# S5 recursion over chunks: scans in a rotating frame in place of a stepwise recursion, in a two-layer hybrid encoder

## The chip, the cores and the metric

One core of one Trainium2 chip runs the whole program. The metric is device time in microseconds from launch to the last output, the median of several executions. Engines are TensorE (PE; its weight loads are shown as PEld), VectorE (DVE), ScalarE (ACT), GpSimd (POOL) and SyncE (SP), which issues the DMAs.

## What is computed

Two sequences (a prompt and a sample, 512 tokens of 1024 channels each) pass through the same two layers. Each layer projects to the inputs of four mixers (S5, Hyena, RWKV-7, neighbourhood attention), normalises and projects their outputs, and ends with an MLP.

```python
def encoder_trunk(x, p):
    for l in range(DEPTH):
        h = rms_norm(x, p['ln1_g'][l])
        z = h @ p['w_in'][l]
        z_s5, z_hy, z_rw, z_na = jnp.split(z, IN_SPLITS, axis=-1)
        groups = [rms_norm(y, g) for y, g in (s5_mixer, hyena_mixer, rwkv_mixer, na_mixer)]
        x = x + jnp.concatenate(groups, axis=-1) @ p['w_out'][l]
        h = rms_norm(x, p['ln2_g'][l])
        x = x + jnp.square(jax.nn.relu(h @ p['w_mlp1'][l])) @ p['w_mlp2'][l]
```

(The four calls are shortened.) S5 is a diagonal complex recursion over the tokens, s[t] = a s[t-1] + B u[t], once forwards and once backwards; 16 groups of 16 channels have 64 states each. The pole is a = exp(lambda dt), that is, a magnitude `mag = exp(lam_re dt)` and an angle `lam_im dt`. The output is the real part of C s.

## The kernel before

Tokens lie along the free dimension, channels along the 128 partitions. Dense products (`mm3`, L1385 to L1395) take fp32 operands in two parts and run three matmuls of 128x512 for each pair of tiles: L1392, L1393 and L1394, 9024 in all. Their weights are split by `split` (L297 on ScalarE, L298 on GpSimd or VectorE), and VectorE takes the results from PSUM (L1449, L1518, L1535, L1545).

The program is written as streams of Python generators whose parts are emitted in turn (`together`, `both`). `dense_stream` runs, for layer l and sequence b, the output projection `w_out` of the mixers' outputs, the MLP and `w_in` of the next layer. `rwkv_stream` runs the mixers: for each (l, b) `rwkv` beside `s5`, then `hyena` beside `na`; after (0, 1) come the operators of layer 1 (`prep`: `s5_ops`, `hy_spectra`). The operators of layer 0, and Hyena and attention of (0, 0), are in `first_stream`. `w_out` of (l, b) waits for the mixers of (l, b), and the mixers of (1, b) wait for `w_in` of (1, b). The framework's scheduler sets the order of instructions on each engine at build time, by the priorities of the emission and its own estimate of when operands are ready; on the chip every engine works through its queue in order.

S5 works in chunks of 8 tokens, so a sequence has 64 chunks. `s5_ops` makes the chunk operators of a layer from its weights and keeps them in DRAM (`sB`, `sC`, `GD`), with a^8 in two small tiles (`AR`, `AI`). `s5_front` (L915) loads the inputs `U`, and for each two pairs of groups the operator `Bop` (L926); 32 matmuls (L933) give every chunk's own contribution in PSUM, ScalarE copies it (L935) into `SS` [128, 2 (re, im), 8 pairs, 130], with the forward chunks at places 1 to 64 and the backward ones at 65 to 128. Then 63 steps go over the chunks, all pairs and both directions at once, four VectorE operations on 32 columns each:

```python
        nc.vector.tensor_tensor(out=t2.rearrange("p q (x d) -> p (q x) d", d=2), in0=pv, in1=AIv, op=MUL)
        nc.vector.tensor_tensor(out=t1, in0=pv, in1=ARv, op=MUL)
        t1f = t1.rearrange("p (q x) d -> p q (x d)", q=2)
        nc.vector.tensor_tensor(out=t1f, in0=t1f, in1=t2[:, ::-1], op=ADD)
        nc.vector.tensor_tensor(out=cv, in0=cv, in1=t1, op=ADD)
```

(L946, L947, L949, L950). The halves of `SS` are then exchanged between partitions by two DMAs, and `s5_back` forms the outputs. A front runs four times, once for each (l, b).

## Time and profile before

| | us |
|---|---|
| median of three runs (lowest, highest) | 3235.25 (3233.89, 3237.98) |
| span of the profiled execution, first to last instruction | 3230.3 |
| PE, DVE, ACT, POOL busy in it | 2989.3, 2222.3, 1054.7, 1222.8 |

The profile is of one execution whose own time is not listed apart from the three; its span lies 4.95 us below their median. Busy time of PE counts pipelined matmuls from start to end, so it says less about how far PE is from its best pace than the count of matmuls in a stretch does.

### The profile page before, as it was taken

To read this page: it belongs to the slowest core of one execution; us is meant where nothing else is said; L and a number is where in the kernel's file an instruction comes from. 1 tells how busy PE (TensorE), PEld (TensorE's weight loads), DVE (VectorE), ACT (ScalarE), POOL (GpSimd) and SP (SyncE) were. 2 spreads that over 40 slices of the span, in tenths; PEclk is the share of its full clock that TensorE was granted. 3 is DMA by queue.
4 is the path that set the end of the run, shared out by engine and by line. 5 is a ranking of instruction groups with operands and counts; after the bars stand their busy time and mean duration, and the time that the engine had idled before them with its cause. 6 is when DMAs were issued, how large, how long until landed. Compare 5 with 4: busy or idle time off the path is not lost.

```text
span 3230.3 us, 48385 instructions
## 1 busy us (share of the span) xinstructions
PE 2989.3 (93%) x17328; PEld 2329.1 (72%) x17328; DVE 2222.3 (69%) x4431; ACT 1054.7 (33%) x1934; POOL 1222.8 (38%) x963
## 2 busy tenths in 40 slices
PE   7998898789899998998889999788999999999999
PEld 5676776667677776676667777677777777888887
DVE  8987993774884879648957366868775486544443
ACT  5333233342222334333222233333332233332222
POOL 6644430332323346453333233443333243343333
PEclk9999888799999999998999999899989999999999
DMA  5464253252334334543324333346234333433333
GB/s 162 145 160 151 98 144 93 74 115 77 89 100 143 92 117 140 153 144 93 90 72 106 102 115 108 105 137 167 76 74 117 111 115 101 126 110 98 95 98 108
DMA packets 361397, 365.23 MB, mean 113 GB/s; under 512 B 175014, under 2 KB 215590, under 8 KB 360136
## 3 DMA queue, kind: packets, MB, share of 16 engines
q1 hardware_dynamic: 361160, 362.14, 38.6%
q8 instruction: 140, 2.29, 0.3%
q14 instruction: 97, 0.79, 0.1%
HBM read 305.06 MB, written 54.10 MB: 111 GB/s over the span
## 4 chain that ended last, share of the span: by engine, by line
PE 39%; DVE 14%; DMA 2%; issue 2%; ACT 1%; SPq 1%; POOL 0%; DVEq 0%; ACTq 0%; POOLq 0%
PE pd L1392 10%; PE pd L1394 10%; PE pd L1393 10%; DVE m L1167 1%; DVE m L298 1%; PE ra L675 1%; DVE m L530 1%; PE ra L673 1%; PE ra L467 1%; DVE m L950 1%; DVE m L512 1%; DVE s_t L946 1%; DVE s_t L949 1%; DVE m L1545 1%; DVE do L1535 0%
## 5 line engine op out<-in xcount | busy, mean ns | idle before, releaser
L298 POOL TENSOR_TENSOR m<-m,m 128x512 fp32r<-128x512 f32 x564 | 793.4, 1409 | 1480.2 <-ACT m L297 1432.4
L1392 PE MATMUL pd<-m,m 128*128 128x512 f32 x2984 | 1225.8, 411 | 108.1 <-ACT m L297 36.0
L1394 PE MATMUL pd<-m,m 128*128 128x512 f32 x2984 | 1212.6, 407 | 14.9 <-POOL m L298 9.8
L1393 PE MATMUL pd<-m,m 128*128 128x512 f32 x2984 | 1211.9, 406 | 2.7 <-DVE m L298 2.1
L297 ACT CAST m<-m 128x512 fp32r<-128x512 f32 (+1 forms) x776 | 488.2, 632 | 1112.8 <-PE pd L1393 401.7
L1392 PEld LDWEIGHTS pd<-m,m 128*128 128x128 f32 x2984 | 581.8, 195 | 264.7 <-issue 68.9
L1394 PEld LDWEIGHTS pd<-m,m 128*128 128x128 f32 x2984 | 581.3, 195 | 160.9 <-POOL m L298 16.3
L1393 PEld LDWEIGHTS pd<-m,m 128*128 128x128 f32 x2984 | 581.4, 195 | 132.8 <-issue 9.1
L1545 DVE TENSOR_TENSOR m<-pd,m 128x512 f32<-128x512 f32 x256 | 175.1, 686 | 234.7 <-PE pd L1394 234.1
L298 DVE TENSOR_TENSOR m<-m,m 128x512 fp32r<-128x512 f32 (+1 forms) x212 | 172.6, 814 | 116.6 <-ACT m L297 116.1
L1535 DVE SCALAR_TENSOR_TENSOR do<-pd,R 128x512 f32<-128x512 f32 x128 | 87.7, 687 | 112.5 <-PE pd L1394 104.3
L297 ACT CAST m<-do 128x512 fp32r<-128x512 f32 x128 | 79.4, 620 | 237.2 <-DVE do L1536 237.1
L1167 DVE TENSOR_TENSOR m<-m,m 128x512 f32<-128x512 f32 (+1 forms) x224 | 154.2, 724 | 1.1 <-POOL m L1167 0.8
L298 DVE TENSOR_TENSOR m<-do,m 128x512 fp32r<-128x512 f32 x128 | 101.5, 794 | 45.1 <-ACT m L297 44.5
L1536 DVE TENSOR_TENSOR do<-do 128x512 f32<-128x512 f32 x128 | 129.5, 1013 | 2.6
L467 PE MATMUL ra<-m,m 64*128 64x128 f32 x512 | 73.4, 335 | 22.1 <-DVE m L451 12.4
L467 PEld LDWEIGHTS ra<-m,m 64*128 64x128 f32 x512 | 62.7, 229 | 37.8 <-issue 20.4
L946 DVE TENSOR_TENSOR s_t<-m,s_AI 128x32 f32<-128x32 f32 x252 | 81.6, 324 | 7.3 <-ACT m L935 1.8
L950 DVE TENSOR_TENSOR m<-m,s_t 128x32 f32<-128x32 f32 x252 | 83.1, 330 | 5.0
L675 PE MATMUL ra<-m,m 128*64 128x64 f32 x512 | 79.0, 248 | 0.0
L840 POOL TENSOR_TENSOR m<-m,s5p_i 128x256 f32<-128x256 f32 x64 | 57.8, 903 | 55.0 <-DVE m L842 31.1
L1423 DVE SCALAR_TENSOR_TENSOR m<-m,par,m 128x512 fp32r<-128x512 f32 x64 | 67.4, 1062 | 15.9 <-ACT m L1422 15.8
(351 smaller groups left out, 3609.5 us busy)
## 6 DMA issues: line engine op xcount, KB each, us to landing
m<-in_w_mlp SPq DMA_DIRECT2D x512, 256.0 KB, 2.6
m<-in_w_in SPq DMA_DIRECT2D x176, 256.0 KB, 2.8
m<-zr SPq DMA_DIRECT2D x36, 512.0 KB, 4.0
m<-in_w_out SPq DMA_DIRECT2D x64, 256.0 KB, 2.9
m<-in_xT SPq DMA_DIRECT2D x32, 256.0 KB, 4.3
zr<-do SPq DMA_DIRECT2D x32, 256.0 KB, 2.1
m<-hy_spec SPq DMA_DIRECT2D x8, 1024.0 KB, 5.1
m<-s_sB SPq DMA_DIRECT2D x16, 512.0 KB, 4.2
```

What stands on the lines that cost most here:

```text
L297: self.nc.scalar.copy(out=hi, in_=x)
L298: eng.tensor_tensor(out=lo, in0=x, in1=hi.bitcast(F32), op=SUB)
L467: nc.tensor.matmul(out=pm[q][:, ch - c2, c], lhsT=bk[c][h, ch].rearrange("p a b -> p (a b)"), rhs=ar[c][h, ch].rearrange("p a b -> p (a b) ...
L675: nc.tensor.matmul(out=py[b0:b0 + 64, d, c], lhsT=uv[:, ch, c, q], rhs=sr[:, ch, 2 * c + q], start=st is None, stop=True)
L946: nc.vector.tensor_tensor(out=t2.rearrange("p q (x d) -> p (q x) d", d=2), in0=pv, in1=AIv, op=MUL)
L950: nc.vector.tensor_tensor(out=cv, in0=cv, in1=t1, op=ADD)
L1167: eng.tensor_tensor(out=o, in0=a, in1=b, op=op)
L1392: K.nc.tensor.matmul(out=ps, lhsT=wh, rhs=hh, start=(i == 0), stop=False)
L1393: K.nc.tensor.matmul(out=ps, lhsT=wh, rhs=hl, start=False, stop=False)
L1394: K.nc.tensor.matmul(out=ps, lhsT=wl, rhs=hh, start=False, stop=(i == n - 1))
L1536: nc.vector.tensor_tensor(out=r, in0=r, in1=r, op=MUL)
L1545: nc.vector.tensor_tensor(out=x[m], in0=ps, in1=x[m], op=ADD)
```

## The change

For each layer `s5_ops` now builds two tables. `E` holds the turns exp(i n theta8) for n = 0 to 63, where theta8 is the angle of a^8, built by doubling in six rounds of four products and sums. `rr` holds the magnitude of a^8 at each of 130 places, with zeros where a direction starts. Both go to DRAM as `TD` [128, 8, 386]. `s5_front` works on one pair of groups at a time: it loads `Bop` and the table, runs 16 matmuls (the backward direction with its chunks reversed, so that both directions run upwards), turns the contributions back by their angle straight from PSUM, runs one real scan each for the real and the imaginary part over 130 places, and turns the result forwards again into `SS`. Each pair gives control back to the other streams twice. Comments and docstrings were taken out as well, so lines behind the tables stand 26 lower than before (L1392 is L1418). The core of the diff:

```diff
@@ s5_ops @@
-    x, y = are, aim
-    for _ in range(3):
+    E, rr = M([P, 2, 16, 64]), M([P, 8, 130])
+    x, y = cs, th
+    for i in range(3):
+        last = i == 2
         x2, y2, xy = (K.t([P, 16], "s5p_" + n, 2) for n in ("x2", "y2", "xy"))
         tt(x2, x, x, MUL)
         tt(y2, y, y, MUL)
         tt(xy, x, y, MUL)
-        tt(x2, x2, y2, SUB)
-        V.tensor_scalar(out=xy, in0=xy, scalar1=2.0, scalar2=None, op0=MUL)
+        tt(E[:, 0, :, 1] if last else x2, x2, y2, SUB)
+        V.tensor_scalar(out=E[:, 1, :, 1] if last else xy, in0=xy, scalar1=2.0, scalar2=None, op0=MUL)
+        tt(mag, mag, mag, MUL)
         x, y = x2, xy
-    r8, i8 = pairs(x, y)
...
+    nc.gpsimd.memset(E[:, 0, :, 0:1], 1.0)
+    nc.gpsimd.memset(E[:, 1, :, 0:1], 0.0)
+    for d in range(2):
+        nc.gpsimd.tensor_copy(out=rr[:, :, 1 + 64 * d:65 + 64 * d],
+                              in_=mag.rearrange("p (g d) -> p d g", d=2)[:, d].unsqueeze(2).to_broadcast([P, 8, 64]))
+    nc.gpsimd.memset(rr[:, :, 0:130:129], 0.0)
+    nc.gpsimd.memset(rr[:, :, 1:66:64], 0.0)
+    for k in (1, 2, 4, 8, 16, 32):
+        n = min(k, 63 - k)
+        t1, t2 = M([P, 2, 16, n]), M([P, 2, 16, n])
+        for t, ri in ((t1, 0), (t2, 1)):
+            tt(t, E[:, :, :, 1:1 + n], E[:, ri, :, k:k + 1].unsqueeze(1).to_broadcast([P, 2, 16, n]), MUL)
+        tt(E[:, 0, :, k + 1:k + 1 + n], t1[:, 0], t2[:, 1], SUB)
+        tt(E[:, 1, :, k + 1:k + 1 + n], t1[:, 1], t2[:, 0], ADD)
+        M.free(t1, t2)
+    TD = K.d([P, 8, 386], f"s5_tb{l}")
+    for ri in range(2):
+        nc.sync.dma_start(out=TD[:, :, P * ri:P * ri + P], in_=E[:, ri].rearrange("p (g x) n -> p g (x n)", g=8))
+    nc.sync.dma_start(out=TD[:, :, 256:386], in_=rr)
@@ s5_front @@
-    for gp in range(0, 8, 2):
-        Bop = M([P, 2, 2, 2, P])
...
-        nc.scalar.copy(out=SS[:, :, gp:gp + 2, 1:129], in_=px)
...
+    for g in range(8):
+        Bop = M([P, 2, 2, P])
+        nc.sync.dma_start(out=Bop.rearrange("p r d n -> p (r d n)"), in_=sB[:, g])
+        tb = M([P, 386])
+        nc.sync.dma_start(out=tb, in_=TD[:, g])
+        px = K.p([P, 2, P], "ma")
...
+        E = [tb[:, P * i:P * i + P].unsqueeze(1).to_broadcast([P, 2, P]) for i in range(2)]
+        t = [M([P, 2, P]) for _ in range(2)]
+        W = SS[:, :, g, 1:129]
+        for i in range(2):
+            V.tensor_tensor(out=t[i], in0=px, in1=E[i], op=MUL)
+        V.tensor_tensor(out=W[:, 0], in0=t[0][:, 0], in1=t[1][:, 1], op=ADD)
+        V.tensor_tensor(out=W[:, 1], in0=t[0][:, 1], in1=t[1][:, 0], op=SUB)
+        for ri in range(2):
+            V.tensor_tensor_scan(out=SS[:, ri, g], data0=tb[:, 256:386], data1=SS[:, ri, g], initial=0.0, op0=MUL, op1=ADD)
+        for i in range(2):
+            V.tensor_tensor(out=t[i], in0=W, in1=E[i], op=MUL)
+        for ri, op in ((0, SUB), (1, ADD)):
+            for d, o in ((0, slice(1, 65)), (1, slice(128, 64, -1))):
+                ns = slice(64 * d, 64 * d + 64)
+                V.tensor_tensor(out=SS[:, ri, g, o], in0=t[0][:, ri, ns], in1=t[1][:, 1 - ri, ns], op=op)
+        M.free(tb, *t)
+        for _ in range(2):
+            yield
```

The built program has 3852 VectorE instructions in place of 4434 and the same 13755 on TensorE, but the scheduler gives both, and the DMAs, another order. On VectorE, in the first front, the order before runs steps of the recursion back to back (`m_2613` is `SS`, `s_t` the step's two products, `do` a dense output):

```order
L946 TENSOR_TENSOR s_t_236_2955<-m_2613,s_AI_142_1778 128x32
L947 TENSOR_TENSOR s_t_235_2954<-m_2613,s_AR_141_1777 128x32
L949 TENSOR_TENSOR s_t_235_2954<-s_t_235_2954,s_t_236_2955 128x32
L950 TENSOR_TENSOR m_2613<-m_2613,s_t_235_2954 128x16x2
L946 TENSOR_TENSOR s_t_238_2961<-m_2613,s_AI_142_1778 128x32
L947 TENSOR_TENSOR s_t_237_2960<-m_2613,s_AR_141_1777 128x32
L316 SCALAR_TENSOR_TENSOR do_4413<-dt_4415,par_67,do_4413 128x512
```

In the changed order the first pair of groups stands there (`ma_2682` is the contribution in PSUM, `m_2680` the table, `m_2691` and `m_2692` the products, `m_2653` is `SS`; the order prints a scan as SCALAR_TENSOR_TENSOR):

```order
L965 TENSOR_TENSOR m_2691<-ma_2682,m_2680 128x256
L965 TENSOR_TENSOR m_2692<-ma_2682,m_2680 128x256
L587 COPY m_1903<-ra_1985 32x8x32
L966 TENSOR_TENSOR m_2653<-m_2691,m_2692 128x128
L967 TENSOR_TENSOR m_2653<-m_2691,m_2692 128x128
L969 SCALAR_TENSOR_TENSOR m_2653<-m_2680,m_2653 128x130 x2
L587 COPY m_1903<-ra_1985 32x8x32
L971 TENSOR_TENSOR m_2691<-m_2653,m_2680 128x256
L971 TENSOR_TENSOR m_2692<-m_2653,m_2680 128x256
L298 TENSOR_TENSOR m_4054<-m_4053,m_4052 128x512
L975 TENSOR_TENSOR m_2653<-m_2691,m_2692 128x64 x4
```

Between two pairs of groups the other streams' operations stand, nine rows of them behind this one.

On TensorE, at the end of the mixers of layer 1, sequence 0, the order before has dense products of `w_in` (`pd`) around the sums and broadcasts of the group norms (L271, L293; `ra_16513` and `ra_16532` are those of the mixer that ends last):

```order
L1393 MATMUL pd_18782<-m_18693,m_18776 128x512
L1394 MATMUL pd_18782<-m_18693,m_18778 128x512
L271 MATMUL ra_16513<-c_ones_131,m_16508 128x1 x4
L293 MATMUL nm_18715<-c_eye_129,rsq_ynm_18703 128x128 x4
L1392 MATMUL pd_18826<-m_18511,m_18814 128x512
L1393 MATMUL pd_18826<-m_18511,m_18814 128x512
L1394 MATMUL pd_18826<-m_18511,m_18816 128x512
```

The changed order has, at the same event, the end of attention's values (L1366, L1372), Hyena's last products (L1274), the group norms and the next front's matmuls (L956) with no dense product among them; the last dense product ahead of them is that of `pd_19680`, and the next one, 33 rows further, is the first of `w_out` (`pd_19815`):

```order
L1274 MATMUL ra_15799<-m_15017,m_15673 128x128
L1274 MATMUL ra_15810<-m_15017,m_15673 128x128
L293 MATMUL ma_15666<-c_eye_129,rsq_yma_15654 128x128 x4
L956 MATMUL ma_19891<-m_19864,m_19887 64x64 x8
L956 MATMUL ma_19990<-m_19864,m_19986 64x64 x8
L271 MATMUL ra_15869<-c_ones_131,m_15864 128x1 x4
L956 MATMUL ma_20102<-m_19864,m_20098 64x64 x8
L956 MATMUL ma_20203<-m_19864,m_20199 64x64 x8
L293 MATMUL ra_15888<-c_eye_129,rsq_yra_15876 128x128 x4
```

This event stands behind 5568 dense matmuls in the changed order and behind 5108 in the order before.

## Rows read from the trace of the kernel before

**Rows 1.** The page's first line: the span.
```profile
span 3230.3 us, 48385 instructions
```

**Rows 2.** Stages: stretch, us, busy us by engine (instructions), granted clock, DMA share, GB/s.
```profile
0.00:604.00 604.00, 532.31 (x3364) 400.23 (x3364) 489.71 (x1126) 214.60 (x402) 251.88 (x213) 0.90 0.46 135
604.00:1446.00 842.00, 771.70 (x4494) 595.39 (x4493) 596.07 (x1167) 280.06 (x512) 329.21 (x264) 0.94 0.39 111
1446.00:2102.00 656.00, 595.48 (x3622) 461.10 (x3621) 461.86 (x937) 205.46 (x393) 227.87 (x173) 0.94 0.36 101
2133.00:2766.00 633.00, 601.29 (x3685) 468.80 (x3684) 454.67 (x913) 202.94 (x385) 221.78 (x172) 0.95 0.38 109
2766.00:3230.00 464.00, 457.53 (x2020) 377.57 (x2019) 204.08 (x265) 137.38 (x222) 174.59 (x129) 1.00 0.36 107
sum 3230.00, PE 2989.31 PEld 2329.12 DVE 2222.25 ACT 1054.66 POOL 1222.76; mean PE 498.22 PEld 388.19 DVE 370.38 ACT 175.78 POOL 203.79
```

**Rows 3.** The same columns: the four recursions, and a stretch without one.
```profile
298.00:484.00 186.00, 170.83 (x971) 134.78 (x971) 176.84 (x476) 54.46 (x107) 68.89 (x61) 0.88 0.40 117
836.00:967.00 131.00, 118.05 (x745) 91.30 (x744) 117.36 (x353) 36.04 (x72) 33.98 (x26) 0.92 0.38 95
1492.00:1620.00 128.00, 110.03 (x728) 84.91 (x727) 118.91 (x364) 39.43 (x77) 37.57 (x26) 0.95 0.36 87
2204.00:2321.00 117.00, 105.49 (x704) 81.52 (x703) 111.23 (x308) 34.68 (x69) 39.94 (x30) 0.90 0.43 122
1650.00:1836.00 186.00, 173.59 (x1159) 133.72 (x1158) 114.56 (x169) 54.20 (x104) 64.53 (x48) 0.97 0.38 99
```

**Rows 4.** Groups of instructions: busy us, mean ns, idle before; the recursion's four.
```profile
L950 DVE TENSOR_TENSOR m<-m,s_t 128x32 f32<-128x32 f32 x252 | 83.1, 330 | 5.0
L946 DVE TENSOR_TENSOR s_t<-m,s_AI 128x32 f32<-128x32 f32 x252 | 81.6, 324 | 7.3 <-ACT m L935 1.8
L949 DVE TENSOR_TENSOR s_t<-s_t,s_t 128x32 f32<-128x32 f32 x252 | 66.8, 265 | 5.4
L947 DVE TENSOR_TENSOR s_t<-m,s_AR 128x32 f32<-128x32 f32 x252 | 59.2, 235 | 0.1
```

**Rows 5.** Single lines: ns min/median/max, first and last start us, forms.
```profile
L946 DVE TENSOR_TENSOR s_t<-m,s_AI x252: 184/208/1325, 298.1 to 2320.1; 128x32 f32<-128x32 f32 x126
L472 DVE TENSOR_TENSOR m<-ra,c_rwmask x128: 403/414/426, 148.6 to 2396.1; 128x256 f32<-128x256 f32 x128
L842 DVE TENSOR_TENSOR m<-m,m x128: 273/284/1397, 30.2 to 1328.1; 128x128 f32<-128x128 f32 x128
L421 DVE TENSOR_TENSOR_SCAN m<-c_rwscan,m x16: 673/692/1806, 117.0 to 2366.7; 128x256 f32<-128x256 f32 x16
L935 ACT COPY m<-ma x16: 566/588/592, 263.5 to 2203.0; 128x512 f32<-128x512 f32 x16
```

**Rows 6.** Groups of instructions, as rows 4: wider VectorE operations.
```profile
L1167 DVE TENSOR_TENSOR m<-m,m 128x256 f32<-128x256 f32 x128 | 72.5, 602 | 1.0 <-POOL m L1167 0.8
L530 DVE TENSOR_TENSOR m<-m 128x1024 f32<-128x1024 f32 x32 | 68.4, 2138 | 5.1 <-DMA m<-m 3.1 <-ACT m L297 1.5 <-ACT m L526 0.4
L842 DVE TENSOR_TENSOR m<-m,m 128x128 f32<-128x128 f32 x128 | 58.3, 495 | 9.3 <-POOL m L840 8.5
```

**Rows 7.** Single lines within stretches, as rows 5: mixers' starts (L343), ends (L293).
```profile
L343 DVE SCALAR_TENSOR_TENSOR m<-m,par,ra x2: 742/744/747, 605.7 to 606.7; 128x512 f32<-128x512 f32 x2
...
L343 DVE SCALAR_TENSOR_TENSOR m<-m,par,ra x2: 742/744/747, 1445.7 to 1446.4; 128x512 f32<-128x512 f32 x2
...
L343 DVE SCALAR_TENSOR_TENSOR m<-m,par,ra x2: 743/746/748, 2132.6 to 2133.3; 128x512 f32<-128x512 f32 x2
...
L293 PE MATMUL ra<-c_eye,rsq_yra x8: 270/272/275, 1915.1 to 2100.7; 128*128 128x128 f32 x8
...
L293 PE MATMUL ma<-c_eye,rsq_yma x8: 272/272/273, 1921.9 to 2080.2; 128*128 128x128 f32 x8
...
L293 PE MATMUL ra<-c_eye,rsq_yra x8: 271/272/322, 2595.9 to 2765.0; 128*128 128x128 f32 x8
```

**Rows 8.** DMA issues: KB each, median us from issue to landing.
```profile
m<-s_sB SPq DMA_DIRECT2D x16, 512.0 KB, 4.2
s_sB<-m SPq DMA_DIRECT2D x16, 256.0 KB, 4.1
```

More of the change, by code (lines that the diff above doesn't have):

```diff
@@ L809, in s5_ops @@
         tt(xy, x, y, MUL)
-        tt(x2, x2, y2, SUB)
-        V.tensor_scalar(out=xy, in0=xy, scalar1=2.0, scalar2=None, op0=MUL)
+        tt(E[:, 0, :, 1] if last else x2, x2, y2, SUB)
+        V.tensor_scalar(out=E[:, 1, :, 1] if last else xy, in0=xy, scalar1=2.0, scalar2=None, op0=MUL)
+        tt(mag, mag, mag, MUL)
         x, y = x2, xy
-    r8, i8 = pairs(x, y)
-    AR, AI = K.t([P, 2, 16], f"s5_AR{l}"), K.t([P, 2, 16], f"s5_AI{l}")
-    V.tensor_copy(out=AR, in_=r8)
-    V.tensor_copy(out=AI, in_=i8)
-    K.s5w[l] = (sB, sC, GD, AR, AI)
+    nc.gpsimd.memset(E[:, 0, :, 0:1], 1.0)
[17 more added lines that the diff above has]
+    nc.sync.dma_start(out=TD[:, :, 256:386], in_=rr)
+    M.free(E, rr)
+    K.s5w[l] = (sB, sC, GD, TD)
     yield
@@ L916, in s5_front @@
     nc = K.nc
-    sB, sC, GD, AR, AI = K.s5w[l]
+    V = nc.vector
+    sB, sC, GD, TD = K.s5w[l]
+    SS = M([P, 2, 8, 130])
+    nc.gpsimd.memset(SS[:, :, :, 0:130:129], 0.0)
     U = M([P, 16, 64])
-    SS = M([P, 2, 8, 130])
     for t in range(8):
         nc.sync.dma_start(out=U[16 * t:16 * t + 16], in_=zd[:, :, t].rearrange("g c n -> c g n"))
-    nc.gpsimd.memset(SS[:, :, :, 0:130:129], 0.0)
     yield
-    for gp in range(0, 8, 2):
-        Bop = M([P, 2, 2, 2, P])
-        nc.sync.dma_start(out=Bop.rearrange("p g r d n -> p g (r d n)"), in_=sB[:, gp:gp + 2])
-        px = K.p([P, 2, 2, P], "ma")
-        for j in range(2):
-            for ri in range(2):
-                for d in range(2):
-                    for q in range(2):
-                        b0 = 64 * q
-                        nc.tensor.matmul(out=px[b0:b0 + 64, ri, j, 64 * d:64 * d + 64], lhsT=Bop[:, j, ri, d, b0:b0 + 64],
-                                         rhs=U[:, 2 * (gp + j) + q], start=True, stop=True)
-        nc.scalar.copy(out=SS[:, :, gp:gp + 2, 1:129], in_=px)
-        M.free(Bop)
-        yield
@@ L938, in s5_front @@
-    ARv = AR.rearrange("p r (g d) -> p (r g) d", d=2)
-    AIv = AI.rearrange("p r (g d) -> p (r g) d", d=2)
-    SV = SS.rearrange("p r g n -> p (r g) n")
-    for i in range(1, 64):
-        pv = SV[:, :, i:130 - i:129 - 2 * i]
-        cv = SV[:, :, 1 + i:129 - i:127 - 2 * i]
-        t1 = K.t([P, 16, 2], "s5_t1", 2)
-        t2 = K.t([P, 2, 16], "s5_t2", 2)
-        nc.vector.tensor_tensor(out=t2.rearrange("p q (x d) -> p (q x) d", d=2), in0=pv, in1=AIv, op=MUL)
-        nc.vector.tensor_tensor(out=t1, in0=pv, in1=ARv, op=MUL)
-        t1f = t1.rearrange("p (q x) d -> p q (x d)", q=2)
-        nc.vector.tensor_tensor(out=t1f, in0=t1f, in1=t2[:, ::-1], op=ADD)
-        nc.vector.tensor_tensor(out=cv, in0=cv, in1=t1, op=ADD)
-        if i % 4 == 0:
+    for g in range(8):
[5 more added lines that the diff above has]
+        for ri in range(2):
+            for d in range(2):
+                for q in range(2):
+                    b0 = 64 * q
+                    u = U[:, 2 * g + q]
+                    nc.tensor.matmul(out=px[b0:b0 + 64, ri, 64 * d:64 * d + 64], lhsT=Bop[:, ri, d, b0:b0 + 64],
+                                     rhs=u[:, ::-1] if d else u, start=True, stop=True)
+        M.free(Bop)
+        E = [tb[:, P * i:P * i + P].unsqueeze(1).to_broadcast([P, 2, P]) for i in range(2)]
[5 more added lines that the diff above has]
+        V.tensor_tensor(out=W[:, 1], in0=t[0][:, 1], in1=t[1][:, 0], op=SUB)
+        for ri in range(2):
+            V.tensor_tensor_scan(out=SS[:, ri, g], data0=tb[:, 256:386], data1=SS[:, ri, g], initial=0.0, op0=MUL, op1=ADD)
[7 more added lines that the diff above has]
+        for _ in range(2):
@@ L966, in s5_back @@
     nc = K.nc
-    sB, sC, GD, AR, AI = K.s5w[l]
+    sB, sC, GD, _ = K.s5w[l]
     U, SS = front
```

## The prediction

> **What bounds the kernel now.** I read the span of 3230.3 us [rows 1] cut into stages first, because one share over the span mixes stages with different limits. The boundaries are events of the mixers' chain. RWKV's k is normalised (L343) where the mixers of a sequence start, and the last group norm broadcast (L293) is where they end: 605.7, 1445.7, 2132.6 for the starts of (layer 0, sequence 1), (1, 0), (1, 1); 2100.7 and 2765.0 for the ends of (1, 0) and (1, 1) [rows 7]. In the last stage TensorE is busy 457.5 of 464 us and VectorE 204 [rows 2]: dense products alone. Before it TensorE leaves 71.7, 70.3, 60.5 and 31.7 us idle in the stages of 604, 842, 656 and 633 us, at a granted clock of 0.90, 0.94, 0.94 and 0.95, against 1.00 in the last one [rows 2]. So most of the time goes to TensorE's work, and what an edit elsewhere can win is idle time of these four stages, 234 us.
>
> Next the four stretches of the recursion [rows 3]. VectorE is busy 176.8 of 186, 117.4 of 131, 118.9 of 128 and 111.2 of 117 us, 90 to 95%. In a stretch of the same length without it, 1650 to 1836, it is 114.6 of 186. TensorE's idle time in the four is 15.2, 13.0, 18.0 and 11.5 us. VectorE is the limit there, or close to it, for the mixers' chain and for the dense products' evictions that queue on it.
>
> **What leaves.** Four groups of 252 small operations, 81.6 + 59.2 + 66.8 + 83.1 = 290.7 us [rows 4], or 72.7 us of VectorE per front, and the copies of L935, 4 x 0.588 us per front on ScalarE [rows 5], which I cost at nothing: ScalarE is busy a third of the time (sum in [rows 2]). The matmuls of L933 stay the same in number. Eight operator loads of 256 KB replace four of 512 KB, and eight table loads of 198 KB come on SP's queue; with the DMA engines' share at 0.36 to 0.46 [rows 2] I cost them at nothing, and their landing is a rival below.
>
> **What comes.** Eight groups per front, each of twelve VectorE operations. Two products from PSUM with 256 columns take 0.414 us each (L472) [rows 5]. Two sums of 128 columns lie between L842's median of 0.284 [rows 5] and its mean of 0.495 [rows 6]. For two scans of 130 places the nearest row is L421, 0.692 for 256 [rows 5]: half is 0.35, the whole the upper bound. Two products of 256 columns in SBUF take from 0.40, about L472's price, to 0.602, the mean of L1167 [rows 6]. Four sums of 64 columns lie between L946's median of 0.208 [rows 5] and its mean of 0.324 [rows 4]. The sum of a group is 3.7 to 5.7 us, a front 30 to 46. I take 37, nearer the low end, because the long prices are means with stalls: L946 runs from 0.184 to 1.325 us and L842 from 0.273 to 1.397, while L472, which reads PSUM, stays within 0.403 to 0.426 [rows 5]. Fewer operations that can stall should stall less. So a front gives VectorE 36 us back (27 to 43).
>
> [...]
>
> Tables, per layer: 24 VectorE operations that double a width from 32 to 992 columns. By L946, L842, L1167 and L530 (2.138 for 1024 columns) [rows 4 to 6] the products come to about 8 us and the sums to 4: 12, with 18 as the upper bound. GpSimd's copies and memsets and three stores on SP's queue stand beside other work: GpSimd is busy 1222.8 of 3230 us (sum in [rows 2]); without that cover they would delay the first front by a store, some 4 us by [rows 8]. In layer 0 the table lies right ahead of the first front and takes back a third of its relief. In layer 1 it lies in the second stage, where VectorE is busy 596 of 842 us [rows 2]: 0 to 12 us, I take 3.
>
> **What moves.** The orders show more than the diff. Counted along TensorE's queue in dense matmuls (9024 in all, in both), the mixers' milestones stand as follows before and now: start of (0, 1) 1152 and 1176; start of (1, 0) 3407 and 3876; end of (1, 0) 5108 and 5568; end of (1, 1) 7013 and 7296. So the second stage takes 445 dense matmuls more and the last one 283 less. TensorE works in order, so this work is moved, not saved: the last stage's pace is 464 us / (9024 - 7013) = 0.2307 us, so 103 us are added to the second stage, 65 leave the last one, 30 leave the 31 us in which the mixers waited for z of (1, 1) [rows 7], and 8 leave the other stages. It gains only if it fills idle time. The second stage is idle 8.3%. If it comes down to the fourth stage's 5.0% (the stage with most dense matmuls per us, 1776 in 633), it fills 70 - 42 = 28 us (0 to 70). There is a price, too. At 5568 nothing dense is left but the output projection that waits for these mixers, and the order puts the whole end of attention and Hyena there. Before, from the one group norm's broadcast (2080.2) to the other's (2100.7), 20.5 us, dense work ran beside it [rows 7]. The same again at 7296: 0 to 41 us of new waiting, I take 20.
>
> The first stage: VectorE is the limit at 95% and 36 - 12 = 24 us leave, of which I take 22 (0 to 43); behind it dense work is short until the mixers are through, so an earlier end counts. The stretches in the third and fourth stage can't give more to TensorE than their idle 18.0 and 11.5 us; two thirds is 12 and 8 (0 to 36 each, if the mixers' chain itself is what VectorE held back). That of the second is within the 28.
>
> **Sum.** 3230 - 22 - 28 - 12 - 8 + 3 + 20 = 3183 us of span. The median of the runs is 4.95 us above the span of the profile, so I forecast **3188 us**, 1.5% less.
>
> By the matmul rows TensorE has 234 us of idle in the four stages. [...]
>
> **Rivals.**
> *The mixers' chain was paced by VectorE and runs free.* For: 90 to 95% in all four stretches [rows 3], and the mixers' wait of 31 us for z is gone. Against: the recursion covers only 562 of the first 2766 us. All the relief arrives, 24 + 24 + 36 + 36 = 120, with 28 filled and 20 waited: 3230 - 128 + 5 = 3107.
> *VectorE is off the path.* TensorE is already busy 92, 90, 86 and 90% in the four stretches [rows 3]; then only moving counts, 28 filled against 20 and 3 paid: 3230 us, the same within measurement.
> *Slower: the output projections wait for mixers that come late.* Mixer matmuls stand behind 445 more dense ones in TensorE's queue. If the second stage's idle time is latency that these don't reach, nothing is filled, both projections wait in full (41) and the tables cost 12; with the first stage's 22 gained: 3230 + 53 - 22 + 5 = 3266. It decides once less than about 25 us of the idle 70 is filled. For it: the order at 5568 shows no dense row between the last products of attention and the projection.
> *Table loads hold VectorE.* VectorE stood idle before the recursion's 1008 operations for 17.8 us in all [rows 4], while each group now waits for its matmuls and a table. A load like L926's lands after 4.2 us [rows 8]: if half of the 32 are exposed with RWKV's work queued behind them, 68 us come on top: 3256. Against: loads are issued a group ahead where memory allows.
>
> **How the numbers follow.** A measurement of this kernel can tell about 0.2% from no change, 6.5 us. Forecast (3150 to 3225) 0.48; chain runs free 0.22; off the path 0.12; late mixers 0.12; table loads 0.06. Faster 0.48 + 0.22 = 0.70, same 0.12, slower 0.18. The range of 8 in 10 runs from 3095 (a third of the free chain lies below) to 3245 (most of the two slow cases lie above).
>
> **What would show it.** Right: VectorE's sum falls from 2222 to about 2100 us (290.7 gone, 148 + 24 added); L343 of (0, 1) starts near 583 instead of 605.7; the second stage is longer but its idle share falls to about 5%; the last stage takes about 400 us. Wrong: VectorE shows idle time in front of the scan groups that a DMA ends; TensorE is idle for more than 40 us in front of the two output projections; or VectorE's sum hardly falls because scans cost the whole 0.69.

## The result, and the profile after

The changed kernel takes 3220.3 us (median of 20 runs, 3204.4 to 3235.9) against 3235.3 us for the kernel before (20 runs): a ratio of 0.9948, interval 0.9934 to 0.9963. In a later set of runs the same pair gave 3230.0 and 3233.4 us, ratio 0.9979 (0.9953 to 1.0004). So it is faster by some 0.2 to 0.5% (the second interval reaches 1), a third of the forecast 1.5% at best. 3188 lies 32 us below what was measured. The first median is inside the range of 8 in 10 and even inside the band of the forecast itself (3150 to 3225); that is luck, since the steps below do not add up as forecast, and the second median, 3230.0, is the time of the rival "VectorE is off the path".

First the page of the changed kernel: its span and the line of sums. VectorE fell by 71.5 us, not by the 120 that were forecast.

```profile
span 3224.4 us, 48021 instructions
PE 2981.8 (92%) x17328; PEld 2321.0 (72%) x17328; DVE 2150.7 (67%) x3849; ACT 1047.7 (32%) x1920; POOL 1229.3 (38%) x975
```

Its stages, with the columns of [rows 2] and, as there, without the short stretch before z of (1, 1); the first boundary is that of [rows 2] and not yet the end of the stage:

```profile
0.00:604.00 604.00, 520.02 (x3324) 389.27 (x3325) 468.18 (x974) 213.43 (x397) 249.40 (x218) 0.90 0.49 139
604.00:1539.00 935.00, 879.61 (x5013) 684.45 (x5012) 653.52 (x1124) 313.77 (x569) 379.09 (x304) 0.96 0.41 115
1539.00:2180.00 641.00, 588.49 (x3665) 456.90 (x3663) 431.42 (x778) 204.02 (x385) 230.16 (x177) 0.94 0.42 121
2195.00:2819.00 624.00, 582.02 (x3504) 451.05 (x3504) 412.69 (x708) 195.04 (x374) 218.70 (x166) 0.94 0.37 104
2819.00:3224.00 405.00, 396.64 (x1742) 326.71 (x1740) 172.66 (x227) 118.16 (x191) 150.67 (x110) 0.99 0.33 97
```

The events that bound the stages answer to [rows 7]: L343 where the mixers of (0, 1), (1, 0) and (1, 1) start, and L293 where those of (1, 0) and of (1, 1) end (2179.7 and 2819.0).

```profile
L343 DVE SCALAR_TENSOR_TENSOR m<-m,par,ra x2: 741/741/741, 620.8 to 621.5; 128x512 f32<-128x512 f32 x2
...
L343 DVE SCALAR_TENSOR_TENSOR m<-m,par,ra x2: 739/741/743, 1539.1 to 1539.7; 128x512 f32<-128x512 f32 x2
...
L293 PE MATMUL ra<-c_eye,rsq_yra x4: 421/422/476, 2179.0 to 2179.7; 128*128 128x128 f32 x4
...
L343 DVE SCALAR_TENSOR_TENSOR m<-m,par,ra x2: 742/742/742, 2195.3 to 2196.0; 128x512 f32<-128x512 f32 x2
...
L293 PE MATMUL ra<-c_eye,rsq_yra x8: 271/347/448, 2661.4 to 2819.0; 128*128 128x128 f32 x8
```

| Stage | before, us | forecast | after |
|---|---|---|---|
| first, to the start of (0, 1) | 605.7 | -22 | 620.8 (+15) |
| second, to the start of (1, 0) | 840.0 | +75 (103 moved in, 28 filled), +3 | 918.3 (+78) |
| third, to the end of (1, 0) | 655.0 | -12, and some of 8 moved out | 640.6 (-14) |
| wait for (1, 1) | 31.9 | -30, and 20 for new waits | 15.6 (-16) |
| fourth, to the end of (1, 1) | 632.4 | -8 | 623.7 (-9) |
| last | 465 | -65 | 405 (-60) |

One row stands out. The second, third, fourth and last stage and the wait came out within some 6 us of the text in length; the first one lengthened by 15 us where 22 were to go, and these 37 us are nearly all of the 41 us between the forecast span (3183) and this one.

### The profile page after: what moved, and what is told of

Same layout as the page of the kernel before. It is cut to its first block, busy times and chain, and to the rows that moved or that the text cites. A ratio compares the mean times of both kernels' runs of the same rounds, so it can differ in the third digit from the quotient of the medians.

```text
span 3224.4 us, 48021 instructions
## 1 busy us (share of the span) xinstructions
PE 2981.8 (92%) x17328; PEld 2321.0 (72%) x17328; DVE 2150.7 (67%) x3849; ACT 1047.7 (32%) x1920; POOL 1229.3 (38%) x975
## 4 chain that ended last, share of the span: by engine, by line
PE 55%; DVE 18%; DMA 7%; issue 3%; SPq 1%; ACT 1%; POOL 1%; DVEq 0%; ACTq 0%; POOLq 0%
PE pd L1418 14%; PE pd L1420 13%; PE pd L1419 13%; DVE m L1193 2%; DVE m L298 2%; PE ra L675 2%; PE ra L673 1%; DMA m<-in_w_mlp 1%; DVE m L530 1%; DVE m L862 1%; PE ra L467 1%; DMA m<-rw_D 1%; DVE m L512 1%; DMA m<-s_tb 1%; DVE m L532 1%
## 5 line engine op out<-in xcount | busy, mean ns | idle before, releaser
L298 POOL TENSOR_TENSOR m<-m,m 128x512 fp32r<-128x512 f32 x564 | 798.6, 1418 | 1425.1 <-ACT m L297 1400.6
L1418 PE MATMUL pd<-m,m 128*128 128x512 f32 x2984 | 1226.4, 412 | 88.1 <-ACT m L297 33.6
L1418 PEld LDWEIGHTS pd<-m,m 128*128 128x128 f32 x2984 | 579.8, 194 | 250.3 <-ACT m L297 60.4
L298 DVE TENSOR_TENSOR m<-m,m 128x512 fp32r<-128x512 f32 (+1 forms) x212 | 179.2, 847 | 95.8 <-ACT m L297 95.2
L298 DVE TENSOR_TENSOR m<-do,m 128x512 fp32r<-128x512 f32 x128 | 118.2, 925 | 65.2 <-ACT m L297 64.6
L467 PE MATMUL ra<-m,m 64*128 64x128 f32 x512 | 66.0, 314 | 25.3 <-DVE m L451 9.9
L467 PEld LDWEIGHTS ra<-m,m 64*128 64x128 f32 x512 | 56.1, 213 | 44.5 <-issue 23.1
L1449 DVE SCALAR_TENSOR_TENSOR m<-m,par,m 128x512 fp32r<-128x512 f32 x64 | 67.5, 1065 | 23.5 <-ACT m L1448 23.4
L1442 POOL TENSOR_TENSOR m<-m 128x512 f32<-128x512 f32 x40 | 58.7, 1466 | 60.5 <-ACT m L1441 50.0
L862 DVE TENSOR_TENSOR m<-m,m 128x128 f32<-128x128 f32 x128 | 67.2, 564 | 12.1 <-POOL m L860 10.8
```

The source lines that it names most:

```text
L298: eng.tensor_tensor(out=lo, in0=x, in1=hi.bitcast(F32), op=SUB)
L467: nc.tensor.matmul(out=pm[q][:, ch - c2, c], lhsT=bk[c][h, ch].rearrange("p a b -> p (a b)"), rhs=ar[c][h, ch].rearrange("p a b -> p (a b) ...
L862: V.tensor_tensor(out=out[:, 4 * q:4 * q + 4], in0=ta[:, 4 * q:4 * q + 4], in1=tb[:, 4 - 4 * q:8 - 4 * q], op=(SUB if conj else ADD))
L1418: K.nc.tensor.matmul(out=ps, lhsT=wh, rhs=hh, start=(i == 0), stop=False)
```

## The experiments

In all the expectations the start of (0, 1) is read from the wait ahead of L343, 1 or 2 us before the row of L343 itself; what was measured is given by that row. One profile is shown of every kernel, and the first stage scatters between profiles: (0, 1) starts at 620.8 and 629.7 in two profiles of the changed kernel and at 612.1 in one whose order is the same up to there (the yield in layer 1 alone, below).

**Memory.** The first suspicion came from SP's queue. The kernel before reads the inverses of the first RWKV step back (L542) right after it has written them (rows: start, us, engine, line, operation):

```profile
220.32 0.63 SPq L538 DMA_DIRECT2D rw_D<-m  x1
222.08 2.75 SPq L542 DMA_DIRECT2D m<-rw_D  x4
```

In the changed kernel 42 us pass between the two, and the stores of the tables stand in between:

```profile
214.55 0.63 SPq L538 DMA_DIRECT2D rw_D<-m  x1
...
242.93 0.56 SPq L835 DMA_DIRECT2D s_tb<-m  x1
251.69 0.33 SPq L947 DMA_DIRECT2D m<-s_sB  x1
256.01 1.27 SPq L834 DMA_DIRECT2D s_tb<-m  x2
257.32 7.22 SPq L542 DMA_DIRECT2D m<-rw_D  x4
```

`rc`, the tile that L542 fills, is given the place of `t1`, `t2` of the last doubling, so it is free only when the tables are done. Four runs were to tell this wait from the tables' own work.

`rc` elsewhere, in the first step alone:

```diff
+    M.tight = Mem.clock > 200
     rc = M([P, 2, 16, 32])
+    M.tight = True
```

> The changed kernel; only the tile rc of the first rwkv step of (0,0), into which L542 reads the inverses back, is given other memory, so that it no longer takes the place of the scratch of the tables' last doubling. Theory M (memory): in the changed kernel this read was issued at 257 us, 42 us after the writes before it (L538, 215 us), because its memory came free only with the last table; with other memory it is issued by 225 us, the rwkv chain of the first stage moves 30 to 35 us up, (0,1) starts at 585 to 605 us instead of 621, and the time is 3183 to 3205 us. Rival T (the tables' own VectorE work holds the stage): the read comes early but (0,1) still starts at 615 to 625, time 3215 to 3225. Rival O (the projections wait for late mixers in layer 1 whatever the first stage does): (0,1) starts early as by M, but the time falls by under 8 us.

The kernel before with the tables made and never read:

```diff
     for half in range(2):
         yield from s5_half(K, l, half, f2, a2, sB, sC, GD, M, tag)
+    E, rr = M([P, 2, 16, 64]), M([P, 8, 130])
...
+    M.free(E, rr)
     # a^8 for the recursion over chunks, laid out (ri, pair, dir)
```

> The kernel before, its 63-step recursion kept, with the tables of both layers made and written and never read. Theory M: rc gets the tables' scratch here too, the read is issued at 250 to 270 us, (0,1) starts 30 to 45 us later than in the kernel before (636 to 650 us), time 3265 to 3280 us. Rival T: the tables cost their own VectorE work, 12 us a layer on a stage that VectorE limits: (0,1) starts at 615 to 625, time 3245 to 3255 us.

The same with the three lines for `rc`:

> The same with other memory for rc in the first step. Theory M: the delay is gone but for the tables' own work: (0,1) starts at 610 to 625, time 3240 to 3255 us, 20 to 35 us below the run with the tables alone. Rival T: as the run with the tables alone, within 5 us.

The changed kernel with the table code ahead of the loop over `half`, and a yield behind the doublings and another behind the stores:

> The changed kernel with the table code moved ahead of the two calls of s5_half, so that the tables are made at the start of the program and their scratch is long free when rc takes memory. Theory M: as with other memory for rc, (0,1) starts at 585 to 610, time 3180 to 3205 us. Rival T: the same VectorE work in the same stage, (0,1) starts at 615 to 625, time 3215 to 3225 us.

| Kernel | L542 issued | (0, 1) starts | time, us | ratio to before |
|---|---|---|---|---|
| changed, `rc` elsewhere | 218.5 | 628.4 | 3240.0 | 1.0020 (0.9992 to 1.0048) |
| before, tables unread | 258 | 627.5 | 3247.4 | 1.0044 (1.0022 to 1.0066) |
| the same, `rc` elsewhere | 219 | 621.9 | 3231.2 | 0.9994 (0.9969 to 1.0020) |
| changed, tables first | 244 | 624.7 | 3235.5 | 1.0010 (0.9986 to 1.0033) |

With `rc` elsewhere the read came early as expected, and the start of (0, 1) did not follow: 628.4 us in the changed kernel, and 621.9 after 627.5 in the kernel with unread tables. In time that second pair differs by 16 us (1.0044 and 0.9994, intervals apart), under the 20 to 35 of theory M and over the 5 of rival T. The changed kernel with `rc` elsewhere is slower than the changed kernel (0.9948 and 0.9979), not faster. In the first kernel of the table VectorE shows why (columns as above, with the number of instructions): the consumer of the read, L550 (L548 in the changed kernel), stands behind the last doublings in VectorE's own order.

```profile
218.50 2.42 SPq L544 DMA_DIRECT2D m<-rw_D  x4
```
```profile
249.38 3.36 DVE L758 TENSOR_TENSOR m<-m 128x992 f32<-128x992 f32 x2
...
254.48 1.25 DVE L758 TENSOR_TENSOR m<-m,m 128x496 f32<-128x496 f32 x2
...
256.40 1.21 DVE L550 TENSOR_TENSOR m<-m,c_blk 128x1024 f32<-128x1024 f32 x1
```

Two things hold over the four. With the doublings in one block, (0, 1) starts at 622 to 628 us whether S5 takes 63 steps or scans. So the tables cost the first stage some 16 to 22 us, and the cheaper recursion shows no gain against it.

**What the recursion is worth.** The next four asked for the ceiling, for the tables' work and for its place.

```diff
     for i in range(1, 64):
...
-        nc.vector.tensor_tensor(out=t2.rearrange("p q (x d) -> p (q x) d", d=2), in0=pv, in1=AIv, op=MUL)
-        nc.vector.tensor_tensor(out=t1, in0=pv, in1=ARv, op=MUL)
...
-        nc.vector.tensor_tensor(out=t1f, in0=t1f, in1=t2[:, ::-1], op=ADD)
-        nc.vector.tensor_tensor(out=cv, in0=cv, in1=t1, op=ADD)
```

> The kernel before with the four VectorE operations of every one of the 63 steps left out (the states are the chunks' inputs, so the output is another one), no tables. It is the ceiling of what any cheaper recursion can bring. Theory C (the rwkv chain of (0,0) sets the end of the first stage, the recursion only fills VectorE beside it): (0,1) starts at 595 to 606 us as before (604), time 3190 to 3230 us. Theory V (VectorE's sum limits the first stage, as the prediction had it): 37 to 74 us of work gone from 298 to 484 us bring (0,1) to 560 to 580, time 3120 to 3170 us.

Measured: 3182.6 us, ratio 0.9849 (0.9816 to 0.9882); (0, 1) starts at 589.8. Time and start lie between the two theories: 7 and 5 us below what C gave, 13 and 10 us above what V gave. This is the most telling run of the study. **A recursion that costs nothing at all wins 1.5%**, what was forecast for one that keeps half of its work. In the first stage 74.5 us of VectorE bring 15.9 us.

```diff
-    for k in (1, 2, 4, 8, 16, 32):
...
+    nc.gpsimd.memset(E[:, :, :, 2:64], 0.5)
```

> The changed kernel with the six doublings of both layers' tables left out (the tables are a constant, written and loaded as in the changed kernel; the output is another one). Theory C: the block of 15 us on VectorE that stood ahead of L548 is gone, L548 runs at 228 to 235 us instead of 268, the rwkv chain is where it was in the kernel before, (0,1) starts at 598 to 608 (620 in the changed kernel), time 3195 to 3212. Theory V: 15 us less work in the first stage and the recursion's relief in full, (0,1) at 575 to 590, time 3175 to 3195.

Measured: 3211.8 us, 0.9947 (0.9923 to 0.9971); L548 at 222, (0, 1) at 604.5, where it was before the change. Start and time speak for C; the start also says that the scans' relief in this stage is no more than the scatter. The ratio is that of the changed kernel itself (0.9948 and 0.9979): a first stage 16 us shorter did not by itself give a run that is clearly faster.

```diff
         M.free(t1, t2)
+        yield
```

> The changed kernel with one line added, a yield after each doubling of the tables, so that other streams' instructions come between the doublings; all work is kept. L548 then stands ahead of the doublings on VectorE, and rc takes memory that the tables do not use. Theory C: as the run without the doublings within 8 us: L548 at 228 to 240, (0,1) starts at 600 to 610, time 3195 to 3215. Theory T (the tables' work counts wherever it stands): as the changed kernel, (0,1) at 616 to 624, time 3215 to 3225.

Measured: 3204.9 us, 0.9925 (0.9898 to 0.9951); L548 at 221, (0, 1) at 615.0. The time is as C gave it, the start is 5 us late for C and just below T.

> The run with a yield after each doubling, and one yield a group instead of two in s5_front, so that a mixer's program comes in fewer turns against the dense stream: on TensorE (0,1) comes after 791 dense matmuls instead of 1092, (1,0) after 3401 instead of 3532. Theory D (dense work that runs ahead of the mixers is worth nothing, since the last stage cannot be under 400 us and starts with the last mixer): (0,1) starts 30 to 60 us earlier than with two yields, the mixers of (1,1) end 10 to 40 us earlier, time 3165 to 3200 us. Rival (the chains set the stages whatever dense does): stages move under 15 us, time within 10 us of the run with two yields.

Measured: 3263.1 us, 1.0100 (1.0078 to 1.0122). (0, 1) does start 41 us earlier, at 574.1, but (1, 0) at 1495.2 against 1496.3: the second stage takes the 41 us back. Theory D falls, and so does its rival. What the run paid is in the last section.

**The same kernels on one chip, and other places for the tables.**

> The changed kernel itself, beside the next runs on one chip. 3215 to 3225 us, (0,1) starts at 618 to 624.

> The changed kernel with the yield after each doubling, beside the changed kernel on one chip. Theory C: 8 to 20 us below it (the 30 to 38 us delay of L548 taken away is worth 6 us at the start of (0,1), and mixers and dense work stay closer together: (1,0) starts after 3532 dense matmuls instead of 3876). Theory T: within 5 us of it.

> The table code ahead of s5_half, with the yield after each doubling. Theory C: the table's 15 us then lie at 25 to 90 us, where the profile of the changed kernel shows VectorE waiting, and not in the block that made the first step of (0,0) 10 us later in the run with the tables first: (0,1) starts at 600 to 612, time 3195 to 3212. Theory T: the work counts wherever it stands, (0,1) at 616 to 626, time 3210 to 3225.

> The doublings on GpSimd instead of VectorE, with the yield after each. Theory C: VectorE is rid of 15 us a layer; as the run without doublings, (0,1) at 600 to 610, time 3195 to 3212. Rival G: GpSimd's slower operations hold its splits of dense operands and the tables come late for the first scan: (0,1) at 615 to 640, time 3215 to 3250.

| Kernel | (0, 1) starts | time, us | ratio to before |
|---|---|---|---|
| changed | 629.7 | 3230.0 | 0.9979 (0.9953 to 1.0004) |
| yield after each doubling | 618.9 | 3207.7 | 0.9901 (0.9874 to 0.9928) |
| tables first, with the yield | 621.9 | 3232.9 | 0.9997 (0.9975 to 1.0019) |
| doublings on GpSimd, with the yield | 657.2 | 3264.9 | 1.0085 (1.0058 to 1.0112) |

The changed kernel lies 5 us above its own expectation. The yield makes it 22 us faster, 2 more than theory C gave. The other two places miss their expectations: with the tables first L548 runs at 232 us and (0, 1) starts at 621.9 all the same. On GpSimd the doublings cost 57 us more than on VectorE; that is rival G, and beyond its range.

**The price of a microsecond in two places of one stage.** Three kernels, all with the yield, change the VectorE work of the first stage alone:

```diff
-        for i in range(2):
+        for i in 6 * (0, 1) if K.fronts == 1 else (0, 1):
             V.tensor_tensor(out=t[i], in0=px, in1=E[i], op=MUL)
```

> The run with a yield after each doubling, with the first two products of each group in the front of (0,0) alone made six times over: 80 more VectorE operations of some 0.41 us, 33 us, between 260 and 450 us; the values are the same. The start of (0,1) is read, 614 and 618 us in the two runs without them. Theory C: as with the recursion left out of the kernel before (74 us less, 14 us gained), a microsecond here is worth 0.2: (0,1) at 617 to 628. Theory V (the prediction's price, one for one): 645 to 653.

```diff
-        for t, ri in ((t1, 0), (t2, 1)):
+        for _ in range(1 if l else 3):
+            for t, ri in ((t1, 0), (t2, 1)):
...
```

> The run with a yield after each doubling, with every doubling of layer 0 made three times over in its place: 30 us more VectorE work around 220 to 290 us; the values are the same. The runs with and without the doublings (603 against 614 and 618) say about 0.9 a microsecond: (0,1) at 635 to 650. If work there is worth no more than in the front: 618 to 626.

```diff
+        if K.fronts == 1:
+            nc.scalar.copy(out=W, in_=px)
+        else:
             for i in range(2):
...
```

> The run with a yield after each doubling, with the products, scans and sums of the front of (0,0) alone left out (a ScalarE copy puts the chunks' inputs in place; the output is another one): 32 us of VectorE less at 260 to 450 us. Theory C: (0,1) at 604 to 614, against 614 and 618. Theory V: 580 to 588.

The three kernels with the yield (both layers, twice, and layer 0 alone) start (0, 1) at 615.0, 618.9 and 611.4, mean 615.1. VectorE's change is the count times the mean of the lines in question, summed.

| Kernel | VectorE, us | (0, 1) starts | for each us |
|---|---|---|---|
| kernel before, no recursion | -74.5 | 589.8 (605.7) | 0.21 |
| front of (0, 0) left out | -43.1 | 609.5 (615.1) | 0.13 |
| front with 80 more products | +28.6 | 628.7 (615.1) | 0.48 |
| doublings of layer 0 three times | +23.4 | 647.4 (615.1) | 1.4 |
| doublings of both layers left out | -15.0 in layer 0 | 604.5 (620.8) | 1.1 |

The times are 3199.1 us (0.9875, two runs alone) with the front left out, 3217.6 (0.9943) with 80 more products and 3234.1 (1.0003) with the doublings made three times, against 0.9925 and 0.9901 with the yield alone.

Theory V misses at both front kernels, by 22 us where the front is left out and by 16 where products are added. The prices are rough: starts of one and the same order differ by up to 18 us, and two of the edits moved dense work as well. Ahead of (0, 1) stand 1083 dense matmuls in the kernels with the yield, with 80 more products and without the doublings, but 1116 with the front left out, 1208 with the doublings three times and 1176 in the changed kernel. So the 1.4 is not the price of VectorE's work alone. Where the counts agree, adding 28.6 us costs 0.48 each, and leaving the doublings out of the kernels with the yield (615.1 and 604.5, for 11.8 to 14.0 us) brings 0.8 to 0.9.

The windows from 300 to 450 us, the stretch of the front, and from 450 to 600 us show where the work goes (columns of [rows 2]). With the yield:

```profile
300.00:450.00 150.00, 135.78 (x853) 105.30 (x852) 124.13 (x243) 40.65 (x70) 56.67 (x47) 0.91 0.43 128
450.00:600.00 150.00, 126.15 (x984) 91.99 (x984) 89.83 (x196) 49.25 (x113) 27.71 (x28) 0.81 0.41 113
```

With 80 more products, VectorE is fuller by 18.7 us in the front's own stretch and TensorE does as much there as before; it falls back behind it, by 60 matmuls and at a lower clock, 0.68 after 0.81:

```profile
300.00:450.00 150.00, 137.05 (x850) 108.01 (x849) 142.82 (x304) 41.59 (x72) 65.86 (x50) 0.94 0.45 130
450.00:600.00 150.00, 118.83 (x924) 86.00 (x924) 80.64 (x190) 42.48 (x100) 23.65 (x24) 0.68 0.36 96
```

With the front left out, VectorE has 40 idle us of 150; TensorE gains 1.3 us of busy time and starts 900 matmuls there where there were 853:

```profile
300.00:450.00 150.00, 137.08 (x900) 108.98 (x899) 110.16 (x191) 45.25 (x80) 66.12 (x52) 0.93 0.46 129
450.00:600.00 150.00, 127.41 (x1005) 94.17 (x1004) 89.00 (x193) 50.50 (x114) 26.88 (x24) 0.84 0.39 110
```

From 450 us on, where RWKV's four chunks follow one another (L637 to L682), VectorE is idle 40 to 46% of the time in all three. So the 95% of busy time in the front did not say what limits the stage: most of that work could go without the stage getting shorter by it.

**Where the yield's 22 us come from.**

> The changed kernel with the yield after each doubling in layer 0 alone. Theory P (what stands ahead of L548 in the first stage decides the order of all that follows: here (1,0) comes after 3506 dense matmuls): as with the yields in both layers, 3200 to 3212 us, the second stage 880 to 892 us. Rival L (layer 1's tables, made in the second stage, were the block that mattered): as the changed kernel, 3218 to 3232 us, the second stage 915 to 926 us.

> The same in layer 1 alone; (1,0) comes after 3854 dense matmuls, as in the changed kernel with 3876. Theory P: as the changed kernel, 3218 to 3232 us, the second stage 910 to 926 us. Rival L: 3200 to 3212 us, the second stage 880 to 895 us.

In layer 0 alone: 3220.2 us, 0.9971 (0.9949 to 0.9993), second stage 873 us. In layer 1 alone: 3235.8 us, 1.0013 (0.9994 to 1.0032), second stage 915 us. The second stage is 7 us below what theory P gave for the one and within it for the other, and the times lie 8 and 4 us above. So the order of the second stage hangs on what stands in the first, as theory P had it. The time does not follow: with the yield in layer 0 alone it lies in the range of rival L, and its ratio is no better than the changed kernel's (0.9948 and 0.9979), though the second stage is 45 us shorter. How much the order moves is plain in the second rows of two profiles from one chip, first the changed kernel, then the one with the yield:

```profile
0.00:630.00 630.00, 552.67 (x3434) 415.45 (x3434) 483.38 (x1008) 221.27 (x410) 253.73 (x222) 0.86 0.48 136
630.00:1553.00 923.00, 864.87 (x4899) 671.36 (x4898) 638.22 (x1088) 305.18 (x556) 376.75 (x300) 0.96 0.41 114
```
```profile
0.00:619.00 619.00, 529.24 (x3332) 394.11 (x3333) 476.21 (x998) 214.15 (x400) 244.04 (x215) 0.88 0.48 136
619.00:1504.00 885.00, 812.08 (x4702) 625.49 (x4701) 596.17 (x1078) 290.60 (x529) 353.54 (x285) 0.95 0.42 116
```

Counted from the rows of the dense matmuls, the second stage holds 2700 of them in the changed kernel, 2449 with the yield and 2255 before. Over the profiles of all the kernels named here its length follows 424 + 0.186 x that count within 10 us, from 2203 (829 us, no recursion) to 2700 (918 and 924). A dense matmul more costs the second stage 0.19 us of its 0.23.

A shorter second stage is therefore not yet a gain: the matmuls that leave it come later. From the start of (1, 0) to the end the kernel with the yield takes 1705 us where the changed one takes 1686, for 345 dense matmuls more. That these cost 19 us and not the 80 of the last stage's pace (0.23 each) is the gain. The third and fourth stage show it, first of the changed kernel, then with the yield: idle TensorE falls from 53 and 41 us to 31 and 35, and the granted clock is 0.97 in both after 0.93 and 0.94.

```profile
1553.00:2214.00 661.00, 607.78 (x3757) 471.84 (x3756) 445.77 (x821) 207.67 (x391) 230.91 (x178) 0.93 0.43 120
2214.00:2835.00 621.00, 579.85 (x3504) 449.20 (x3503) 412.80 (x707) 194.82 (x374) 218.06 (x166) 0.94 0.38 104
```
```profile
1504.00:2153.00 649.00, 618.50 (x3802) 482.52 (x3801) 457.54 (x797) 215.28 (x408) 243.64 (x186) 0.97 0.41 116
2153.00:2768.00 615.00, 580.41 (x3604) 453.08 (x3604) 414.14 (x733) 196.62 (x377) 219.47 (x169) 0.97 0.38 107
```

Over the whole of these two profiles idle time is the same, 238.5 and 238.0 us, since the first two stages idle more with the yield. The 30 us between them are TensorE's busy time, 3001.4 and 2972.1 us for the same matmuls, at a granted clock of 0.935 and 0.952. In the other pair of profiles (the first of each kernel) 14 of 20 us are idle time and 6 busy time.

**Memory of their own for the tables.** In the kernels with the yield `rc` is free early, but `v`, the next tile of the same step, has the place of the last doubling's scratch. The last run takes layer 0's tables and their scratch out of the shared memory:

```diff
-    E, rr = M([P, 2, 16, 64]), M([P, 8, 130])
+    MT = K.mem((0, DHI)) if l == 0 else M
+    E, rr = MT([P, 2, 16, 64]), MT([P, 8, 130])
...
-        t1, t2 = M([P, 2, 16, n]), M([P, 2, 16, n])
+        t1, t2 = MT([P, 2, 16, n]), MT([P, 2, 16, n])
```

> The changed kernel with the tables of layer 0 and their scratch in the dense stream's part of the memory; no yield added, no work left out. Theory M2 (the tables cost the first stage what the rwkv chain waits for memory that it shares with them: in the changed kernel rc and then v take the scratch of the last doubling, in the run with other memory for rc alone rc's products and in the runs with the yield v take its place): no tile of the first rwkv step waits for a table, L542 is issued by 225 us, v's load by 255 us, the first product with v comes by 260 (283 in the changed kernel), (0,1) starts at 598 to 608 (612 to 630 in three profiles of the changed order), time 3195 to 3212 us. Rival W (the 15 us of VectorE work count by themselves): (0,1) at 612 to 625, time 3212 to 3230 us.

```profile
170.00 0.56 SPq L836 DMA_DIRECT2D s_tb<-m  x1
177.28 1.26 SPq L835 DMA_DIRECT2D s_tb<-m  x2
...
229.14 2.74 SPq L542 DMA_DIRECT2D m<-rw_D  x4
...
240.28 1.07 SPq L322 DMA_DIRECT2D m<-zr  x1
249.13 0.38 SPq L322 DMA_DIRECT2D m<-zr  x1
```

Measured: 3212.9 us, 0.9914 (0.9885 to 0.9943). No read waits for a table: the stores are out at 178 us, both loads of L322 by 250, and the first product with `v` comes at 253. Yet (0, 1) starts at 622.2, and the time is just above what M2 gave: M2 has the loads, rival W has the stage and the time. Against the changed kernel the second stage is shorter again, 875 us with 2467 dense matmuls.

## Why the prediction failed, step by step

**Front and table prices: right.** Four fronts take 156.9 us (counts times means), 39.2 each, forecast 37 (30 to 46). Groups of instructions of the changed kernel, as in [rows 4]:

```profile
L969 DVE TENSOR_TENSOR_SCAN m<-m,m 128x130 f32<-128x130 f32 x64 | 33.2, 549 | 0.0
L971 DVE TENSOR_TENSOR m<-m,m 128x256 f32<-128x256 f32 x64 | 29.6, 501 | 0.4
L975 DVE TENSOR_TENSOR m<-m,m 128x64 f32<-128x64 f32 x128 | 26.7, 266 | 0.3
L965 DVE TENSOR_TENSOR m<-ma,m 128x256 f32<-128x256 f32 x64 | 24.2, 415 | 22.0 <-DMA m<-s_tb 14.3 <-PE ma L956 7.6
```

The doublings take 27.9 us for both layers, forecast 24. The waits for table loads come to 14.3 us over the run, so the rival in which they hold VectorE (68 us) did not come. VectorE's sum missed by 50 us for other reasons: 23 of them are the splits on VectorE (L298), 297 us after 274 for the same 340 instructions; the rest is open.

**The first stage: wrong, by 37 us.** The failed step reads "VectorE is the limit at 95% and 36 - 12 = 24 us leave, of which I take 22". The front gave 31 us back (74.5 before, 43.4 now), but at the 0.13 to 0.21 us that the two runs with work taken out paid for each, that is 4 to 7 us and not 36. The tables' 15.0 us, at the 0.8 to 1.1 of the run without doublings, are 12 to 17. Together that makes 5 to 13 us longer; 15 was measured, and the other two profiles have 6 and 24. The rival "VectorE is off the path" was nearest for the front's work, but it has no term for the tables, which cost about their length.

The 37 us name the stage in which the sum failed, not what a better first stage would have been worth. Without the doublings it is 16 us shorter, at a ratio of 0.9947; with one yield a group it is 47 us shorter and the run 1.0% slower than the kernel before. So the text's "an earlier end counts" did not hold either: the 41 us that the one yield moved out of this stage came up in the next.

**Stages two to four and the last: lengths right, their terms only in part.** The 445 dense matmuls came in and 283 left the last stage, as read from the order, and this carries the two large numbers (+78 and -60). But the added matmuls brought 93 us of busy time and not 103, and filled 15 of the 70 idle us and not 28: idle TensorE came to 55 us of 918 where the text had 42. That 93 - 15 meets 103 - 28 + 3 is luck; the other profile has +84. In the fourth stage nothing was filled: idle time rose from 31.7 to 42.0 us, and the stage is 9 us shorter only because its busy time fell by 19, with 76 dense matmuls fewer. In the third 8 of the forecast 12 us were filled. The new wait in front of the output projection is there: for 42 us TensorE runs no dense product, and 20 of them are idle, in front of the first projection alone; the granted clock of the 62 us shown is 0.70.

```profile
2133.00:2195.00 62.00, 41.98 (x275) 36.03 (x273) 41.44 (x118) 13.34 (x22) 12.50 (x12) 0.70 0.35 115
```

**What remains open.** Why the tables cost the first stage about their length is not settled. Three waits that carry it in the traces (`rc`'s memory, VectorE's order at L548, `v`'s memory) were taken away, and (0, 1) still started at 611 to 628. That the stage has several chains of nearly the same length is a guess that no run tests, and every one of these edits also moved the order. Nor is it explained why a moved matmul is cheap in one order and dear in another, nor how far the lower clock is a cause or only goes with the idle time. The kernel with the tables first ends some 30 us later than the two with the yield; its profile has 6 to 10 us of them in the first stage, 2 to 6 in the second and 12 to 14 behind it.

**A version that beats both:** the yield after each doubling in both layers, 0.9925 and 0.9901 of the kernel before on two chips; memory of their own for the tables comes to 0.9914.

## What to carry to other kernels

A busy share of 95% in a stretch did not mean here that the stage waits for that engine: 74.5 us of VectorE's work taken out made the first stage 15.9 us shorter. Before you credit a cheaper operation one for one, leave it out altogether and see what the ceiling is. Here one run would have said 1.5% for all of it. Price new preparatory work by itself: fifteen microseconds of tables cost the first stage some 10 to 20 in each of the places on VectorE that were tried, and the cheaper loop gave back 4 to 7. And where a planner sets the order, count the moved work along the limiting engine's queue: that number gave most of the second stage's growth. It does not give the time, since what leaves one stage has to fit into another; one `yield` that shifted it was worth more than the new algorithm, and the same `yield` in one layer alone was worth nothing that the runs can tell.

## What the runs showed of the hardware

**Long and short of the same operation.** Single lines of the changed kernel, as [rows 5]:

```profile
L965 DVE TENSOR_TENSOR m<-ma,m x64: 386/415/426, 276.1 to 2234.8; 128x256 f32<-128x256 f32 x64
L971 DVE TENSOR_TENSOR m<-m,m x64: 408/419/1508, 279.0 to 2239.6; 128x256 f32<-128x256 f32 x64
L969 DVE TENSOR_TENSOR_SCAN m<-m,m x64: 390/416/1503, 277.7 to 2238.2; 128x130 f32<-128x130 f32 x64
```

The product that takes one operand from PSUM never took over 426 ns (mean 415, above); the one with both operands in SBUF (mean 501) and the scan (mean 549) took now and then 1.5 us. The long ones have company: of the 64 scans 10 took over 1.3 times the median, and beside all 10 a GpSimd instruction ran, but beside only 7 of the other 54; for the product in SBUF it is 5 of 5 and 11 of 59. Beside 23 of the 64 products from PSUM one ran too, and none of them got longer. That GpSimd is the cause was not shown: no run tests it, and the counts do not tell which of the GpSimd instructions read SBUF. A scan of 130 places took as long as a product of 256 columns (medians of 416 ns, and of 415 and 419).

**A starved TensorE and a lower clock.** In the run with one yield a group the dense stream is starved in the first stage (576 matmuls are through at 492 us, against 281 with two yields), and the granted clock of that stage is 0.79, against 0.87 and 0.88 in the two profiles with two yields:

```profile
0.00:574.00 574.00, 478.15 (x3024) 357.25 (x3025) 439.92 (x962) 192.05 (x367) 215.95 (x197) 0.79 0.46 128
```

Over the run TensorE is busy 3017 us at 0.930, against 2975 at 0.950 with two yields, for the same matmuls; idle are 246 and 229 us. So 42 of the 59 us by which this kernel is slower are longer busy time for the same work, beside a lower clock; 17 are idle time. Between runs of one kernel time and clock go together as well: the changed kernel took 3241.6 us at 0.935 and 3210.9 at 0.946.
